# A hybrid decoder layer on one Trainium2 core: the prompt's mLSTM packed into five tiles of one projection, six of that projection's tiles as Strassen pairs, operand sums in two passes

## The chip, the cores and the metric

The kernel runs on one core of one Trainium2 chip. The metric is device time in microseconds of one launch; three runs of the kernel before gave a median of 2462.95 us. One further execution was profiled, and every duration in the prediction comes from it.

A core has TensorE (PE; PEld is its weight load), VectorE (DVE), ScalarE (ACT), GpSimd (POOL) and SyncE (SP), which here only issues DMA transfers. POOL issues DMA transfers too. Each engine works through its own queue in order and waits there for what its next instruction needs. SBUF is the memory on the chip, PSUM its accumulator memory, eight banks of which TensorE writes and VectorE and ScalarE read.

## What is computed

One inference step of one layer, for a prompt of 512 tokens and a batch of 8 × 4 sample tokens, in fp32. Cut to what matters here:

```python
def _merge(x, h_m, o_m, z_m, h_a, z_a, g_m, g_a, ...):
    ...
    br_m = hn.reshape(B, T, M_WIDTH) * jax.nn.sigmoid(o_m) * jax.nn.silu(z_m)
    br_a = h_a * jax.nn.silu(z_a)
    y = (jax.nn.sigmoid(g_m) * jnp.einsum('btc,cd->btd', br_m, w_proj_m)
         + jax.nn.sigmoid(g_a) * jnp.einsum('btc,cd->btd', br_a, w_proj_a))
    out = jnp.einsum('btc,cd->btd', y, w_out)
    return _layernorm(DN_ALPHA * x + out, ln_w, ln_b)
```

The step first multiplies the 544 tokens by `w_in` (2048 × 18952), which yields q, k, v of two branches and all gates. The attention branch gives `h_a` (sliding window, sinks), the mLSTM branch gives `h_m`: per head (four, of width 512) scores of keys and queries under exponential decays, their product with the values, a normaliser, a layernorm, and the new matrix memory C. Then come three 2048 × 2048 projections: `w_proj_a` on the attention branch, `w_proj_m` on the mLSTM branch, and `w_out` on the gated sum.

## The kernel before

All activations lie with channels on the 128 partitions and the 544 tokens along the free axis. To keep fp32 precision, each operand of a product is split into a high part (a cast to fp32r by ScalarE, line 200 for weights, 245 for activations) and a low part (source minus high part, by VectorE, lines 201 and 246), and a product is three matmuls: high × high, high × low, low × high.

A *plain* tile (`gemm`, line 224, with `products`, line 205) makes 128 output columns. It loads two halves of weights (512 KB each, in three buffers `raw`), splits them, and runs 16 k × 3 matmuls × 2 column halves of 272 tokens = 96 matmuls into two PSUM banks from the pool `psA`. Every so many k (`every`) it calls `tick()`, which lets each of the background generators in `live` trace its next step at that place of the program.

A *Strassen pair* (`paired`, line 718) makes two tiles with seven products of half size in place of eight. Each product (`half_product`, line 677) is 16 + 8 matmuls into one bank. `prepare` (line 658) makes the sums of weights, some on VectorE and some by accumulating DMA transfers from POOL, and splits them; `gather` (line 689) collects the results, partly on POOL (line 704). The right-hand operands of a pair are four quarters of the activations and four sums of quarters, called s1, n2, n3 and s4: products 1 and 2 (counted from 0) use s1 and n2, products 4 and 5 use n3 and s4.

The order of instructions on each engine is made when the program is built, by a scheduler with its own model of durations: each instruction has a priority by its place in the program, `tc.high_priority(offset)` moves it ahead, and `tc.issue_after` ties it behind another one.

The part in question is the last quarter of the time. The branch `d_bra` is split into 8 activation tiles (`branch`, line 1367). Then 16 plain tiles of `w_proj_a` run (line 1555), each loading its gate `d_sga`, multiplying the result by it (line 1560) and storing to `d_t`. Beside them the prompt's mLSTM is a background generator (`mlstm`, line 1506) with one step in each tick, two k apart. For each head it transposes the values (`values`, line 1414) and keys (`keys`, line 1422) through PSUM tiles of the pool `psB`, makes C (line 1438), the scores (line 1470), the weighted values (line 1483), a layernorm, and turns the rows back (line 1493) into `d_brm`. Both PSUM pools hold four banks. When the mLSTM is done, its SBUF is closed, and `d_brm` is read back and split beside the remaining plain tiles.

Then the projection by `w_proj_m`: four plain tiles, five pairs, two plain tiles. Beside the four plain tiles `operand_sums` (line 1574) makes the sums of quarters. It has eight items; an item k loads rows k and k + 8 of the source (544 KB, a transfer issued by POOL, line 1578) into one of two buffers `tx`, makes four sums on VectorE (lines 1587 to 1590) and splits each (four casts, four subtractions of 272 columns), with two ticks to an item. The load for item k + 2 is traced after item k. The projection by `w_out` begins the same way, with sums of `d_y` (line 1674).

Of the kernel before, what the change touches and what calls it, by code (L numbers as in the profile page):

```python
# [25 lines left out]
T = SEQ + NS  # L26
# [48 lines left out]
def _build(tc, nc, i, o, es):  # L75
# [3 lines left out]
    def pool(stack, name, bufs, space=None, side=None):  # L79
        kw = {"space": space} if space is not None else {}  # L80
        if space is None:
            kw["side"] = side or "right"
            kw["reuse_waits"] = "tile"
        return stack.enter_context(tc.tile_pool(name=name, bufs=bufs, **kw))
# [9 lines left out]
    psB = pool(es, "psB", 4, PSUM)  # L94
    psA = pool(es, "psA", 4, PSUM)

    dr = pool(es, "dr", 1, bass.MemoryType.DRAM)
# [3 lines left out]
    def nm(s):  # L101
        count[0] += 1
        return f"{s}_{count[0]}"

# [71 lines left out]
    d_y = dr.tile([16, 128, T], F32, name="d_y")  # L176
    d_o = dr.tile([12, 128, T], F32, name="d_o")
# [46 lines left out]
    def gemm(wv, c0, xh, xl, cols=EVEN, raws=(None, None), every=8, prio=0, before=None, parts=(1, 1),  # L224
             ps=None, behind=None):
        ps = ps or mm()
        for half in range(2):
# [9 lines left out]
            products(ps, half, wh, wl, xh, xl, cols, every)  # L237
# [480 lines left out]
    def paired(work, plain=None):  # L718
# [6 lines left out]
        for at, (w, n) in enumerate(steps):  # L725
# [11 lines left out]
            if n == 2 and "early" in w:  # L737
                w["early"]()
            half_product(w, n)
# [642 lines left out]
    _, bah, bal, g_ = branch(d_bra, act, lambda k: ev(), ahead)  # L1382
# [18 lines left out]
    def f5(dt=F32):  # L1401
        return wA2.tile([128, 512], dt, tag="f5", name=nm("f"))

# [18 lines left out]
    def keys(h, c, kt):  # L1422
# [19 lines left out]
        V.tensor_copy(co[:, 256:512], p1[:, 0:256])  # L1442
# [19 lines left out]
    def cells(h, kh, kl, qh, ql):  # L1462
        hns = []
        for bs_ in ((0,), (1,), (2, 3)):
# [10 lines left out]
            yield  # L1475
        for js in ((0, 1), (2,), (3,)):
            for j in js:
# [9 lines left out]
                hns.append(hn)  # L1487
            yield
        gt = load4(d_g, h)
# [16 lines left out]
    def mlstm():  # L1506
        for h in range(MH):
            vts = load4(d_v, h)
            spawn(decays(h))
            yield  # L1510
            kts = load4(d_k, h)
# [3 lines left out]
            kh, kl, qh, ql = [], [], [], []  # L1515
            g_ = None
            for c in range(4):
                a, b_ = t5(F32R), t5(F32R)
                V.tensor_copy(a[:], kts[c][:])
                V.tensor_tensor(out=b_[:], in0=kts[c][:], in1=r32(a[:]), op=ALU.subtract)  # L1520
                kh.append(a)
                kl.append(b_)
                n_ = keys(h, c, kts[c])
                next(n_)
                if g_ is not None:
# [4 lines left out]
            for c in range(4):  # L1530
                a, b_ = t5(F32R), t5(F32R)
                hilo(qts[c][:], a[:], b_[:])
                qh.append(a)
                ql.append(b_)
# [3 lines left out]
            yield from cells(h, kh, kl, qh, ql)  # L1538
# [15 lines left out]
    bmh = None  # L1554
    for ct in range(16):
        sg = c5t()
        nc.sync.dma_start(sg[:], d_sga[ct])
        ps = gemm(wa_, ct * 128, bah, bal, every=2)
        for p_, s_ in halves(ps, sg):
            V.tensor_tensor(out=s_, in0=p_, in1=s_, op=ALU.mult)  # L1560
        nc.sync.dma_start(d_t[ct], sg[:])
        if bmh is None and (not live or ct == 15):
            drain()
            esA.close()
            es3, esE = ExitStack(), ExitStack()
            act3 = pool(es3, "act3", 8)
            bm_, bmh, bml, g_ = branch(d_brm, act3, lambda k: c5t() if k % 2 else ev())
            spawn(g_)
            c6 = pool(esE, "c6", 2)
            esR = ExitStack()  # L1570
            wr2, pe_ = pool(esR, "wr2b", 3), pool(esR, "peb", 1)
            tx = pool(esR, "txb", 2)
    drain()
    def operand_sums(src, to, p):

        def load(k):
            t_ = tx.tile([128, 2, T], F32, tag="tx", name=nm("tx"))
            G.dma_start(out=t_[:], in_=src[k:k + 9:8].rearrange("k p t -> p k t"))
            return t_

# [353 lines left out]
```

## Time and profile before

| what | value |
|---|---|
| three runs: median (lowest to highest) | 2462.95 us (2462.81 to 2464.43) |
| the profiled execution: its time / its span | 2464.16 us / 2462.4 us |
| mean granted TensorE clock | 0.997 |
| HBM traffic | 169 GB/s over the span |

The chain of work that ended last, by engine (shares of the span) and the costliest lines of it:

```profile
PE 94%; DMA 3%; DVE 2%; issue 1%; ACT 1%; SPq 0%; DVEq 0%; POOL 0%; ACTq 0%; POOLq 0%
```

How to read the rows: times are microseconds unless marked ns, and count from the start of the span. A group row has the line of the kernel, the engine, the operation, `out<-in` by the program's names, shapes, the count; then busy time and mean ns of one; then the idle time of the engine just before these instructions and what ended it (`<-`). A timeline row has start, length, engine, line, operation; idle time before it stands in brackets. Matmuls overlap: one that lasts 0.29 us starts 0.125 us after the one before.

### The profile page before, as it was taken

What the parts mean: (1) busy time and instruction counts of PE and PEld (TensorE: products, weight loads), DVE (VectorE), ACT (ScalarE), POOL (GpSimd) and SP (SyncE); (2) the same over time, 40 slices, a digit from 0 to 9 for tenths busy, and PEclk for the clock granted to TensorE, in tenths of its full rate; (3) what the DMA queues carried; (4) which work ended last, traced back from release to release, by engine and by line L of the source; (5) the groups of instructions that cost most, each with busy time, mean ns of one, the idle gap of its engine ahead of it and who ended that gap; (6) DMA issues with size and microseconds to landing.
All of it is one profiled execution on the core that took longest, in us unless ns stands there. A gap on an engine that the chain in (4) does not pass through costs nothing.

```text
span 2462.4 us, 48812 instructions
## 1 busy us (share of the span) xinstructions
PE 2433.8 (99%) x19446; PEld 2378.9 (97%) x19446; DVE 1884.0 (77%) x2813; ACT 1215.4 (49%) x1994; POOL 509.9 (21%) x478
## 2 busy tenths in 40 slices
PE   8999999999999999999999999999999999999997
PEld 8999999999999999999999999999999999999996
DVE  7768888888888887787887888878855654767657
ACT  5456676676676564433433444544633333344431
POOL 3114334334333331211121122210000000110111
PEclk9999999999999999999999999999999999999998
DMA  6866666666666644578587687576755546888876
GB/s 177 201 173 158 163 161 144 162 161 150 160 154 160 155 124 138 143 217 247 179 242 244 163 241 229 176 251 217 246 171 173 187 147 210 226 218 253 220 221 188
DMA packets 557436, 464.72 MB, mean 189 GB/s; under 512 B 45592, under 2 KB 454344, under 8 KB 556952
## 3 DMA queue, kind: packets, MB, share of 16 engines
q1 hardware_dynamic: 540312, 402.09, 55.1%
q0 software_dynamic: 15696, 57.15, 12.1%
q8 instruction: 153, 2.51, 0.4%
q10 hardware_dynamic: 1200, 2.36, 0.3%
q14 instruction: 75, 0.61, 0.1%
HBM read 319.06 MB, written 96.31 MB: 169 GB/s over the span
## 4 chain that ended last, share of the span: by engine, by line
PE 94%; DMA 3%; DVE 2%; issue 1%; ACT 1%; SPq 0%; DVEq 0%; POOL 0%; ACTq 0%; POOLq 0%
PE bank L685 46%; PE bank L687 23%; PE bank L210 11%; PE sm L1438 2%; PE sm L210 1%; PE bank L1250 1%; PE sm L1470 1%; PE sm L795 1%; PE sm L1483 1%; PE sm L841 1%; DMA tx<-d_y 1%; DMA ty<-d_y 1%; DMA raw<-in_w_in 1%; PE sm L1800 1%; PE sm L821 1%
## 5 line engine op out<-in xcount | busy, mean ns | idle before, releaser
L200 ACT CAST wh<-raw 128x1024 fp32r<-128x1024 f32 x632 | 662.7, 1049 | 836.2 <-PE bank L685 686.6
L201 DVE TENSOR_TENSOR wl<-raw,wh 128x1024 fp32r<-128x1024 f32 x632 | 792.2, 1255 | 194.6 <-ACT wh L200 175.3
L685 PE MATMUL bank<-xk,wh 128*128 128x272 f32 x2336 | 322.7, 289 | 0.0
L665 DVE TENSOR_TENSOR raw<-raw,raw 128x1024 f32<-128x1024 f32 x238 | 304.1, 1279 | 12.6 <-DMA raw<-in_w_in 8.3
L685 PEld LDWEIGHTS bank<-xk,wh 128*128 128x128 f32 x2336 | 303.0, 188 | 2.8 <-issue 2.4
L704 POOL TENSOR_TENSOR ev<-p,ev 128x272 f32<-128x272 f32 x82 | 117.9, 1438 | 458.3 <-ACT ev L703 401.2
L685 PE MATMUL bank<-n2h,wh 128*128 128x272 f32 x656 | 169.8, 291 | 0.2 <-ACT wh L200 0.2
L687 PE MATMUL bank<-xk,wl 128*128 128x272 f32 x1168 | 169.7, 288 | 0.0
L685 PE MATMUL bank<-n3h,wh 128*128 128x272 f32 x656 | 169.6, 291 | 0.0
L685 PE MATMUL bank<-s1h,wh 128*128 128x272 f32 x656 | 169.1, 291 | 0.0
L685 PE MATMUL bank<-n2l,wh 128*128 128x272 f32 x656 | 167.7, 288 | 0.0
L685 PE MATMUL bank<-n3l,wh 128*128 128x272 f32 x656 | 167.6, 288 | 0.0
L685 PE MATMUL bank<-s1l,wh 128*128 128x272 f32 x656 | 167.3, 287 | 0.0
L685 PE MATMUL bank<-s4h,wh 128*128 128x272 f32 x656 | 167.2, 289 | 0.0
L685 PE MATMUL bank<-s4l,wh 128*128 128x272 f32 x656 | 167.0, 287 | 0.0
L687 PEld LDWEIGHTS bank<-xk,wl 128*128 128x128 f32 x1168 | 155.6, 188 | 0.1
L685 PE MATMUL bank<-a11h,wh 128*128 128x272 f32 x584 | 150.6, 290 | 0.0
L685 PE MATMUL bank<-a11l,wh 128*128 128x272 f32 x584 | 149.4, 288 | 0.0
L210 PE MATMUL bank<-bh,wl 128*128 128x272 f32 x704 | 147.5, 290 | 0.7 <-DVE wl L201 0.7
L210 PE MATMUL bank<-bh,wh 128*128 128x272 f32 x704 | 148.1, 289 | 0.0
L210 PE MATMUL bank<-bl,wh 128*128 128x272 f32 x704 | 148.0, 289 | 0.0
L663 POOL DMA_DIRECT2D raw<-raw x90 | 78.1, 868 | 291.8 <-DVE ev L712 202.2
(493 smaller groups left out, 5670.4 us busy)
## 6 DMA issues: line engine op xcount, KB each, us to landing
raw<-in_w_in SPq DMA_DIRECT2D x296, 512.0 KB
raw<-raw POOLq DMA_DIRECT2D x90, 512.0 KB, 4.8
C<-in_state_mlstm_C SPq DMA_DIRECT2D x32, 1024.0 KB
out<-C SPq DMA_DIRECT2D x64, 512.0 KB
raw<-in_w_proj_a SPq DMA_DIRECT2D x32, 512.0 KB
raw<-in_w_proj_m SPq DMA_DIRECT2D x32, 512.0 KB
raw<-in_w_out SPq DMA_DIRECT2D x32, 512.0 KB
d_v<-ev SPq DMA_DIRECT2D x16, 272.0 KB
```

The lines of the kernel that those rows point to most:

```text
L200: state["cast"] = A.copy(wh[:, k:k + n], raw[:, k:k + n])
L201: state["split"] = V.tensor_tensor(out=wl[:, k:k + n], in0=raw[:, k:k + n], in1=r32(wh[:, k:k + n]), op=ALU.subtract)
L210: PE.matmul(ps[f][:, :w], a[:, kk], b(k, c, w), start=(k == 0 and n == 0), stop=(k == 15 and n == 2))
L663: G.dma_start(out=w[out][:], in_=w[b][:], accum_op=ALU.add)
L665: V.tensor_tensor(out=w[out][:], in0=w[a][:], in1=w[b][:], op=ALU.add)
L685: PE.matmul(ps, wh[:, k], x(p, k), start=(first and k == 0 and p == 0), stop=False, skip_group_check=True)
L687: state["end"] = PE.matmul(ps, wl[:, k], x(0, k), start=False, stop=(k == 7), skip_group_check=True)
L704: G.tensor_tensor(out=c22, in0=p1, in1=c11, op=ALU.subtract)
L795: PE.matmul(pp[:, c0 + w0:c0 + 256], qs[a][:, j * 128:j * 128 + 128], kx[:, k0:k0 + 256 - w0], start=(n == 0), stop=(n == 1))
L821: PE.transpose(pt[:, b * 128:b * 128 + 128], s_[:, b, 128:256], ident)
L841: PE.matmul(po[:, b * 128:b * 128 + n], VA[:, b], p_[:, 2 * b:2 * b + n // 128], start=(b == 0 and m == 0), stop=(b == 3 and m == 1), skip ...
L1438: PE.matmul(pp[:, 0:258], a[:, b * 128:b * 128 + 128], b_[:, b, f], start=(b == 0 and n == 0), stop=(b == 3 and n == 2))
```

## The change

PSUM pools can be closed and opened anew: six banks for `psB` and two for `psA` from the start of the `w_proj_a` projection on, four and four again before its pairs. The mLSTM runs beside the first five tiles, with a tick after every k in the first half of a tile and after every second k in the second half. Its loads of the next head's v and k and of the gate are traced earlier, its output rows become a generator of their own (`rows_out`) that runs beside the next head, two of its VectorE copies become ScalarE's, and one step of waiting is dropped. Three plain tiles follow (5 to 7) with the operand sums of `d_bra` beside them, then three pairs (tiles 8 to 13), then two plain tiles (14 and 15) with the reading back of `d_brm`. `operand_sums` has sixteen items in two passes: the first makes n2 and s1 from a full load and stores n2 to `d_n2` in HBM; the second loads three parts again, n2 among them, and makes n3 and s4. Each item is two sums, one cast and one subtraction of 544 columns. It is also the form used for `w_proj_m` and `w_out`, with one tick to an item.

```diff
+    def psum_pools(n):
+        return pool(esPS, nm("psB"), n, PSUM), pool(esPS, nm("psA"), 8 - n, PSUM)
...
-    def paired(work, plain=None):
+    def paired(work, plain=None, rest=()):
...
+            if at == 4:
+                for _ in rest:
+                    pass
             half_product(w, n)
...
+    esPS.close()
+    psB, psA = psum_pools(6)
...
         A.copy(co[:, 0:256], p0[:, 0:256])
-        V.tensor_copy(co[:, 256:512], p1[:, 0:256])
+        A.copy(co[:, 256:512], p1[:, 0:256])
...
+        if h + 1 < MH:
+            pre["v"] = load4(d_v, h + 1)
+        gt = load4(d_g, h)
         for js in ((0, 1), (2,), (3,)):
...
+            if js[-1] == 3 and h + 1 < MH:
+                pre["k"] = load4(d_k, h + 1)
+            yield
+        spawn(rows_out(h, hns, gt))
+
+    def rows_out(h, hns, gt):
...
+            def two_parts(src, to):
+                a, b_ = t5(F32R), t5(F32R)
+                hilo(src[:], a[:], b_[:])
...
-                V.tensor_copy(a[:], kts[c][:])
-                V.tensor_tensor(out=b_[:], in0=kts[c][:], in1=r32(a[:]), op=ALU.subtract)
...
+                two_parts(kts[c], (kh, kl))
...
+    def operand_sums(src, to, p, pace=1):
+        e, f = ([[p.tile([128, 4, 2, HT], F32R, tag="act", name=nm("sum" + n)) for _ in range(2)] for n in "hl"]
+                for _ in range(2))
...
+        def load(k):
+            t_ = tile4()
+            G.dma_start(out=t_[:].rearrange("p (a c) t -> p a (c t)", a=2), in_=src[k:k + 9:8].rearrange("k p t -> p k t"))
+            return t_
+
+        def again(k):
+            t_ = tile4()
+            G.dma_start(out=t_[:, 0:2].rearrange("p c t -> p (c t)"), in_=src[k])
+            G.dma_start(out=t_[:, 2], in_=src[k + 8][:, 0:HT])
+            G.dma_start(out=t_[:, 3], in_=d_n2[k])
+            return t_
+
+        work = [(load, k) for k in range(8)] + [(again, k) for k in range(8)]
+        ahead = [load(0), load(1)]
+        for n, (of, k) in enumerate(work):
+            for _ in range(pace if n < 12 else 1):
+                yield
+            t_ = ahead.pop(0)
+            if of is load:
+                V.tensor_tensor(out=t_[:, 3], in0=t_[:, 3], in1=t_[:, 1], op=ALU.subtract)
+                V.tensor_tensor(out=t_[:, 0], in0=t_[:, 0], in1=t_[:, 3], op=ALU.subtract)
+                nc.sync.dma_start(d_n2[k], t_[:, 0])
+                hilo(t_[:, 0:4:3], e[0][k // 4][:, k % 4], e[1][k // 4][:, k % 4])
+            else:
+                V.scalar_tensor_tensor(t_[:, 1], t_[:, 0], -1.0, t_[:, 1], op0=ALU.mult, op1=ALU.subtract)
+                V.tensor_tensor(out=t_[:, 2], in0=t_[:, 2], in1=t_[:, 3], op=ALU.subtract)
+                hilo(t_[:, 1:3], f[0][k // 4][:, k % 4], f[1][k // 4][:, k % 4])
+            if n + 2 < len(work):
+                nxt, k_ = work[n + 2]
+                ahead.append(nxt(k_))
...
+        return dict(wv=wa_, x=XA, cA=ct * 128, cB=ct * 128 + 128, scale=1.0, acc=True, end=end, early=early)
+
+    LEAD_A, PAIR_A, TAIL_A = 5, 8, 14
+    for ct in range(LEAD_A):
+        plain_a(ct, every=(1, 2))
     drain()
...
+    tx = pool(esR, "txb", 2)
+    SA = {}
+    sums_ = operand_sums(d_bra, SA, act3, 2)
+    next(sums_)
+    spawn(sums_)
+    for ct in range(LEAD_A, PAIR_A):
+        plain_a(ct, every=2, prio=AHEAD)
+    esPS.close()
+    psB, psA = psum_pools(4)
+    XA = operands((bah_, bal_), SA)
+    paired([pair_a(ct) for ct in range(PAIR_A, TAIL_A, 2)], state["split"], rest=sums_)
+    state["end"] = None
+    drain()
+    bm_, bmh, bml, g_ = branch(d_brm, act3, lambda k: ev() if k % 5 < 3 else c6t())
+    spawn(g_)
+    for ct in range(TAIL_A, 16):
+        plain_a(ct, every=2, prio=AHEAD)
+    drain()
```

More of the change, by code (lines that the diff above doesn't have):

```diff
@@ L1556, in _build, with operands, c6t, plain_a @@
+    def operands(tiles, sums):
+        low = [t[2:] for t in tiles]
+        return [side_by_side(tiles, 0), sums["s1"], sums["n2"], side_by_side(low, 0),
+                sums["n3"], sums["s4"], side_by_side(low, HT)]
+    def c6t():
+        return c6.tile([128, T], F32, tag="c6", name=nm("c6"))
+    def plain_a(ct, **kw):
         sg = c5t()
[L1557 to L1558 removed]
+        with tc.issue_after(state["load"].ins):
+            nc.sync.dma_start(sg[:], d_sga[ct])
+        ps = gemm(wa_, ct * 128, bah, bal, **kw)
```

105 lines of the change are left out of this document (45 added, 60 removed).

## The prediction

> **What bounds the kernel now.** I read the page's busy shares first, then the windows by stage, then TensorE's own order of time.
>
> ```profile
> span 2462.4 us, 48812 instructions
> ...
> PE 2433.8 (99%) x19446; PEld 2378.9 (97%) x19446; DVE 1884.0 (77%) x2813; ACT 1215.4 (49%) x1994; POOL 509.9 (21%) x478
> ```
>
> The windows cut the part that the change touches: tiles 0 to 10 of the attention projection with the mLSTM beside them, the rest of that projection, then the four plain tiles of the second and of the third projection with operand sums beside them. Columns: stretch, length, busy time of each engine (instructions), granted clock, share of the DMA engines, GB/s.
>
> ```profile
> 1757.10:2014.10 257.00, 256.30 (x2041) 253.91 (x2040) 161.10 (x401) 99.28 (x190) 10.62 (x20) 1.00 0.53 176
> 2014.10:2078.50 64.40, 64.40 (x520) 64.40 (x519) 30.38 (x46) 22.17 (x31) 0.00 (x0) 1.00 0.70 214
> 2078.50:2126.70 48.20, 48.20 (x387) 48.20 (x386) 35.45 (x72) 18.05 (x35) 5.29 (x7) 1.00 0.78 232
> 2256.70:2305.00 48.30, 47.55 (x382) 47.33 (x381) 37.18 (x78) 22.91 (x49) 5.26 (x7) 1.00 0.82 229
> ```
>
> TensorE idles 0.7 us in the first, nothing in the second and third, 0.75 us in the last. So here time is won only by fewer matmuls and lost by whatever makes TensorE wait.
>
> **Step 1: the matmuls that go.** The timeline of TensorE shows a Strassen product (16 + 8 matmuls) and then plain ones:
>
> ```profile
> 1754.07 2.17 PE L685 MATMUL bank<-xk,wh 128*128 128x272 f32 x16
> 1756.07 1.17 PE L687 MATMUL bank<-xk,wl 128*128 128x272 f32 x8
> 1757.08 0.41 PE L210 MATMUL bank<-bh,wh 128*128 128x272 f32 x2
> ...
> 2077.60 0.41 PE L210 MATMUL bank<-bh,wh 128*128 128x272 f32 x2
> 2077.84 0.41 PE L210 MATMUL bank<-bl,wh 128*128 128x272 f32 x2
> 2078.09 0.42 PE L210 MATMUL bank<-bh,wl 128*128 128x272 f32 x2
> 2078.35 0.41 PE L210 MATMUL bank<-bh,wh 128*128 128x272 f32 x2
> ```
>
> A product takes 1757.08 − 1754.07 = 3.01 us, so a pair (seven) 21.07. Six plain matmuls take 0.75 us, so a tile (96) 12.03 with the 125.4 ns of the product's matmuls, and two tiles 24.07. Three pairs save 3 × 3.0 = **9.0 us**. A pair's VectorE work is seven splits, two weight sums, four gathers and two gate products. With VectorE's durations of lines 201, 1560 and 246 in the next fence that is 9 × 1.22 + 4 × 0.43 + 2 × 0.72 = 14.1 us in 21, hidden; uncovered it would cost 14.1 − 6.6 (the four splits and four evacuations of two plain tiles) = 7.5 us a pair.
>
> **Step 2: the mLSTM in five tiles.** The last stretch of the projection holds 64.4 / 12.03 = 5.35 tiles, the first 10.65, or 128 us; the mLSTM's own TensorE time is thus 257 − 128 = 129 us. Five tiles and the mLSTM: 60 + 129 = 189 us. VectorE's 161 us of the first stretch hold 21 weight splits and gate products, of which five tiles keep ten; 11 × (1.22 + 0.43) = 18 us go, and so do the groups of lines 1442 and 1519 below, which move to ScalarE (6.8 and 6.7):
>
> ```profile
> L201 DVE TENSOR_TENSOR wl<-raw,wh 128x1024 fp32r<-128x1024 f32 x33 | 40.2, 1219 | 18.7 <-ACT wh L200 18.6
> ...
> L1560 DVE TENSOR_TENSOR c<-bank,c 128x272 f32<-128x272 f32 x32 | 12.6, 430 | 12.4 <-PE bank L210 12.2
> ...
> L1442 DVE COPY f<-sm 128x256 f32<-128x256 f32 x16 | 6.8, 422 | 24.1 <-PE sm L1438 24.1
> ...
> L1519 DVE CAST t<-t 128x512 fp32r<-128x512 f32 x16 | 6.7, 420 | 1.5 <-DMA t<-d_k 1.5
> ...
> L246 DVE TENSOR_TENSOR bl<-ev,bh 128x544 fp32r<-128x544 f32 x8 | 5.6, 720 | 1.5 <-ACT bh L245 1.4
> ...
> L245 ACT CAST bh<-ev 128x544 fp32r<-128x544 f32 x8 | 5.0, 647 | 4.0 <-DMA ev<-d_brm 3.9
> ```
>
> About 130 of 189 us stay on VectorE and at most 99 + 14 on ScalarE: covered, cost 0. The loads of the next head's v and k go out earlier on SP's queue and may wait there for tiles, with weights behind them; a half of weights is wanted only every 19 us there, so 0 again, and a few us if that slack goes.
>
> **Step 3: two banks for a plain tile.** The bank pool falls from four to two for tiles 0 to 7, and a tile needs two. The next tile cannot start until VectorE has read both: 0.29 us to the end of the last matmul, two reads of 0.43, and on average half a 1.2 us split in front, less 0.125 of overlap: 1.3 us. At the ends of tiles 0 to 4 an mLSTM step stands between (24 matmuls of an output block, or a score block), and hides it. Tiles 5 and 6 have only operand sums beside them: 2 × 1.3 = **2.6 us**. Bounds: 0, if VectorE's reads come just in time, to 7 × 1.9 = 13 (all seven ends, a whole split in front). [...]
>
> **Step 4: operand sums in sixteen items instead of eight, on the same two buffers.** This decides. It happens three times: new for the attention projection, and changed for the second and third projections, where the pace rises from one item in two ticks (6 us) to one in each (3 us). Old items, in the tile view, and what a load takes:
>
> ```profile
> L1587 DVE TENSOR_TENSOR tx<-tx x16: 429/441/444, 1965.4 to 2298.6; 128x272 f32<-128x272 f32 x16
> ...
> L245 ACT CAST s1h<-tx x16: 413/420/422, 2068.6 to 2299.1; 128x272 fp32r<-128x272 f32 x16
> ...
> DMA to landing us min/median/max: 3.9/6.3/9.0
> ...
> tx<-d_brm POOLq DMA_DIRECT2D x8, 544.0 KB, 6.8
> ...
> tx<-d_y POOLq DMA_DIRECT2D x8, 544.0 KB, 5.2
> ```
>
> With two buffers a load starts only when the item two before it is done. POOL's timeline in the third projection shows that: each load was held by the last sum of the item in its buffer, and the chain of waits runs through the loads.
>
> ```profile
> 2265.50 0.72 POOL L1578 DMA_DIRECT2D tx<-d_y  x1 [8.82 <-DVE s4l L246]
> 2267.48 0.72 POOL L1578 DMA_DIRECT2D tx<-d_y  x1 [1.26 <-DVE s4l L246]
> 2275.83 0.72 POOL L1578 DMA_DIRECT2D tx<-d_y  x1 [7.63 <-DVE s4l L246]
> 2278.95 0.72 POOL L1578 DMA_DIRECT2D tx<-d_y  x1 [2.40 <-DVE s4l L246]
> ...
> 2265.50 7.81 DMA tx<-d_y x2
> ...
> 2278.95 14.23 DMA tx<-d_y x2
> ```
>
> So a buffer's cycle was 10.3 and 11.5 us, and two items came out of each. The new cycle, from rows: landing 5.2 (the lower of the two medians), start 0.2, two VectorE operations 0.9, then a 544-wide cast 0.65 and subtraction 0.72 with 0.2 of hand-over. In the first pass the store of the partial sum must land before the buffer is free; no row gives a 136 KB store, so I bound it by 1.6 (hidden behind cast and subtraction) and 5.2 (a load four times as large), and take 3.3, in between, because it is smaller than the load but starts on SP's queue behind weight loads. First pass 5.2 + 0.2 + 0.9 + 3.3 = 9.6. In the second pass three transfers replace one, POOL's issues 0.72 each, of which I charge one: 5.2 + 0.7 + 0.2 + 0.9 + 1.6 = 8.6. Two items are loaded ahead and take 3.5; then three cycles of the first and four of the second kind: 3.5 + 28.8 + 34.4 = **66.7 us** for a set of sums. With 3.9 for the landing and the store hidden it is 3.5 + 3 × 6.6 + 4 × 7.3 = 52.5; with 6.8 and 5.2 it is 3.5 + 3 × 13.1 + 4 × 10.2 = 83.6.
>
> When must it be done? The fifth product of the first pair reads the last of the second pass, at its eighth k, 1.75 us in. In the second and third projections that is 48.2 + 4 × 3.01 + 1.75 = 62 us after the first plain matmul. In the second projection the low parts go where the old operand's high parts of k 8 to 11 lie, which are read until a quarter before the end of the last tile, 3 us before: 66.7 − 3 − 62 = 1.7 us of waiting. In the third the first sum came 3.2 us after the stage's start:
>
> ```profile
> 2259.89 0.43 DVE L1587 TENSOR_TENSOR tx<-tx 128x272 f32<-128x272 f32 x1
> ```
>
> 66.7 + 3.2 − 62 = 7.9. In the attention projection only three plain tiles lie ahead, 36.1 + 2.6 + 12.0 + 1.75 = 52.5 after the mLSTM's tiles come free: 66.7 − 52.5 = 14.2. Together **23.8 us**. Where the wait appears I leave open: at the fifth product, or earlier, if VectorE stands at a late load with weight splits behind it; either way the set's length is what counts. Bounds of the sum: 0 (52.5 each), and 31 + 19 + 25 = 75 (83.6 each).
>
> [...]
>
> **Step 5: what moves at no charge.** Each set loads 544 KB eight times more and stores 136 KB eight times, 5.6 MB: over 62 us 90 GB/s on top of 230, which is why I don't take the shortest landing. POOL's queue gets the second-pass loads among the pair's accumulating transfers and the subtraction that waits for ScalarE:
>
> ```profile
> POOL ev L704 <- ACT ev L703: 401.2, 53, 22.8
> ```
>
> A load behind that wait is late too; it's inside the upper bound. The mLSTM's gated branch is read back in tiles 14 and 15: 16 × (0.65 ScalarE, 0.72 VectorE), 11.5 us of VectorE in 24 beside four splits and evacuations, hidden, since the plain tiles of the next projection want its k one by one.
>
> **The sum.** The profiled execution took 2464.16 us (span 2462.4 and 1.8 around it), 1.2 above the median of the runs. 2464.2 − 9.0 + 2.6 + 23.8 = 2481.6; less 1.2: **2480 us**, 0.7% slower.
>
> **Rivals.** *The loads keep up (faster).* If landing stays near its 3.9 and the store hides, a set takes 52.5 us and nobody waits: 2463 − 9.0 + 2.6 = 2457. For it: shorter VectorE work per item (2 operations and one wide subtraction for 3.5 us of eight), and the attention stage moves fewer bytes now (0.70 share). Against: the old third set, at half the pace, already had its chain of waits in the loads. It decides from a mean cycle below about 7.2 us (of 9.0 in my sum), and is the case on the other side.
>
> *Half of it (no change).* Cycles between 7.2 and 8.2 us: at 7.9 the attention projection alone waits, 58.8 − 52.5 = 6.3 us, and the gain is spent: 2463. For it: the medians include loads beside many others. Against: my 9.0 leaves nothing for the weight splits that stood between the sums of the old sets.
>
> *The mLSTM does not fit.* A head now takes 63 us, the distance of its score blocks in the chain of waits:
>
> ```profile
> 1796.30 7.54 PE sm L1470 x48
> ...
> 1859.62 7.59 PE sm L1470 x48
> ```
>
> It would get 189 / 4 = 47. If the chain scores, layernorm, transposes needs 50, its tiles are freed 12 us later, and the new sums with them; TensorE goes on with plain tiles but meets the sums 12 us later: 2480 + 12 = 2492. For it: small VectorE and POOL steps in a row. Against: the next head's loads and the row output now overlap it.
>
> *Fewer products don't appear*, since seven for eight are counted in the code: no chance given.
>
> **Chances.** Loads too slow (forecast) 0.49; mLSTM late as well 0.10; half 0.13; loads keep up 0.28. A run of this kernel tells about 0.2% (5 us) from no change. Faster 0.28, same 0.13, slower 0.59. The forecast's own range is 2467 to 2500 (mean cycles of 8.2 to 10, seven to a set). The range to hold the time reaches down to the gain kept whole, 2454, and up to 2500, leaving out cycles beyond 10 us in all three sets.
>
> **What would show it.** Right: TensorE idle in the attention projection's first pair, ended by casts or subtractions of n3 or s4, 10 us or more; POOL's second-pass loads held by the item two before; set lengths (first sum to last subtraction) near 67 us. Step 1 is right if the pairs' products stand at 3.01 us, step 3 if gaps of about 1.3 us end on VectorE's gate product. Wrong: TensorE without gaps at the first pairs, set lengths under 55 us, or idle time inside tiles 0 to 4.

## The result and the profile after

The kernel with the change takes 2537.9 us (four runs, 2536.4 to 2538.3) against 2463.7 before: ratio 1.030, 95% interval 1.0282 to 1.0318. It is slower, as forecast, but by 74 us and not by 17, and outside the range of 2454 to 2500.

The page of the changed kernel, span and busy shares:

```profile
span 2536.1 us, 49009 instructions
...
PE 2454.0 (97%) x19374; PEld 2388.0 (94%) x19374; DVE 1914.3 (75%) x2818; ACT 1244.9 (49%) x2028; POOL 564.4 (22%) x567
```

TensorE has 72 matmuls fewer, three pairs with one product of 24 matmuls saved in each, and is busy 20 us longer. Fewer matmuls in more time is a matter of the granted clock, 0.66 to 1.00 in the windows that follow. Columns as in the prediction. A projection ends here with its last store. The rows are the attention projection in three parts (up to its first pair, the first pair, the rest), then the second projection, then the third with the end of the kernel:

```profile
1757.00:1990.00 233.00, 228.62 (x1811) 225.37 (x1811) 145.97 (x367) 108.81 (x220) 13.01 (x22) 1.00 0.58 188
1990.00:2050.00 60.00, 33.98 (x160) 27.47 (x159) 31.25 (x52) 15.31 (x22) 19.81 (x32) 0.66 0.67 198
2050.00:2121.00 71.00, 69.06 (x553) 68.84 (x552) 44.59 (x60) 30.69 (x43) 6.91 (x7) 1.00 0.86 246
2121.00:2310.00 189.00, 180.78 (x1416) 179.13 (x1416) 127.82 (x181) 71.80 (x91) 32.47 (x45) 0.99 0.88 248
2310.00:2536.00 226.00, 194.44 (x1431) 190.24 (x1429) 135.57 (x204) 65.09 (x87) 36.32 (x50) 0.92 0.74 211
```

The second and third projection of before (the rows of its attention projection stand in the prediction, 257.00 + 64.40 = 321.4 us):

```profile
2078.50:2258.70 180.20, 180.20 (x1442) 180.20 (x1441) 126.84 (x191) 73.44 (x105) 21.70 (x23) 1.00 0.84 235
2258.70:2462.00 203.30, 185.98 (x1439) 184.04 (x1437) 136.11 (x220) 67.38 (x103) 24.16 (x26) 0.97 0.74 208
```

The attention projection is 42.6 us longer (233 + 60 + 71 = 364 against 321.4), the second 8.8, the third 22.7. Counted by matmuls, some 4 us of the 42.6 belong to the second projection: the last matmul of tile 15 ends at about 2116 and its store stands at 2120.9, where before it was 2077.6 and 2078.5. The second row is the one to see: in the 60 us of the first pair TensorE did 160 matmuls, which at the 125.4 ns of before take 20 us. Of the 40 us lost, 26 are idle, and 14 went into matmuls at a granted clock of 0.66. The waits of TensorE say what it stood for (us in total, times, longest):

```profile
PE bank L692 <- ACT sumh L252: 29.6, 14, 4.8
PE bank L217 <- DVE wl L208: 8.6, 6, 3.3
PE bank L692 <- ACT wh L207: 6.6, 4, 2.2
PE bank L692 <- DVE suml L253: 5.5, 8, 1.5
...
PE bank L217 <- DVE c L1630: 0.5, 1, 0.5
```

The high and low parts of the operand sums end 35 us of waiting in all, and the casts and splits of weights another 15, in plain tiles (217) and in products (692): in the second projection all waits, 8.3 us, are of this second kind. There VectorE stood at a sum whose load had not landed, with the weight splits behind it, and ScalarE at the cast of that sum, with a cast of weights behind it. One such place (first VectorE, then ScalarE), after which TensorE waits 0.76 us for a split at 2123.45:

```profile
2119.30 0.44 DVE L1603 TENSOR_TENSOR tx<-tx 128x272 f32<-128x272 f32 x1 [4.37 <-DMA tx<-d_brm]
...
2120.26 0.65 ACT L252 CAST sumh<-tx 128x544 fp32r<-128x544 f32 x1 [7.75 <-DVE tx L1604]
2120.81 1.05 ACT L207 CAST wh<-raw 128x1024 fp32r<-128x1024 f32 x1
```

VectorE's gate product, for which the prediction gave 2.6 us, ends one gap of 0.5.

How long a set of sums took is in the tile view of its subtractions (duration in ns, first and last start), one row for each projection:

```profile
L253 DVE TENSOR_TENSOR suml<-tx,sumh x16: 714/724/726, 1970.9 to 2039.8; 128x544 fp32r<-128x544 f32 x16
...
L253 DVE TENSOR_TENSOR suml<-tx,sumh x16: 718/720/726, 2111.8 to 2190.5; 128x544 fp32r<-128x544 f32 x16
...
L253 DVE TENSOR_TENSOR suml<-tx,sumh x16: 716/719/726, 2314.1 to 2391.0; 128x544 fp32r<-128x544 f32 x16
```

From the first subtraction to the end of the last (in the third projection from the first sum, at 2311.3), 70, 79 and 80 us; the forecast was 67, with bounds of 52.5 and 83.6. In the first two projections the sums of the first two items had been made long before (from 1762.8 and 2042.5 on) and waited for memory. POOL's timeline of the third projection shows why (start, duration, in brackets the idle time before and what ended it; line 1586 is a load of the first pass):

```profile
2315.79 0.72 POOL L1586 DMA_DIRECT2D tx<-d_y  x1 [8.13 <-DVE suml L253]
2317.67 0.72 POOL L1586 DMA_DIRECT2D tx<-d_y  x1 [1.16 <-DMA d_n<-tx]
2327.77 1.44 POOL L1586 DMA_DIRECT2D tx<-d_y  x2 [9.38 <-DMA d_n<-tx]
2341.40 1.44 POOL L1586 DMA_DIRECT2D tx<-d_y  x2 [12.19 <-DMA d_n<-tx]
```

Two loads go out every 12 to 13.6 us, and what they wait for is the store of the partial sum out of the buffer (`d_n<-tx`). The prediction gave this cycle 9.6 us. In the chain of waits (start, length, what ran) loads and stores alternate in the first pass:

```profile
1972.66 7.04 DMA tx<-d_bra
1979.70 8.92 DMA d_n<-tx
...
1998.06 1.74 DMA d_n<-tx
...
2322.86 4.34 DMA d_n<-tx
...
2333.98 6.85 DMA d_n<-tx
```

Six stores stand in the chain; they held their buffers for 1.7, 1.7, 2.3, 4.3, 6.9 and 8.9 us. The prediction put in 3.3, with bounds of 1.6 and 5.2. Around the longest (1979 to 1990) the DMA engines moved 274 GB/s, around the first of the two shortest (1997 to 2001) 111.

### The profile page after: what moved, and what is told of

It reads as the page before. It is cut to its first block, busy times and chain, and to the rows that moved or that the text cites. A ratio compares the mean times of both kernels' runs of the same rounds, so it can differ in the third digit from the quotient of the medians.

```text
span 2536.1 us, 49009 instructions
## 1 busy us (share of the span) xinstructions
PE 2454.0 (97%) x19374; PEld 2388.0 (94%) x19374; DVE 1914.3 (75%) x2818; ACT 1244.9 (49%) x2028; POOL 564.4 (22%) x567
## 4 chain that ended last, share of the span: by engine, by line
PE 85%; DMA 8%; issue 3%; DVE 2%; ACT 1%; POOL 0%; DVEq 0%; SPq 0%; POOLq 0%; ACTq 0%
PE bank L692 45%; PE bank L694 23%; PE bank L217 3%; PE sm L1451 2%; DMA tx<-d_n 2%; PE bank L1260 1%; PE sm L217 1%; DMA tx<-d_y 1%; PE sm L1483 1%; PE sm L805 1%; PE sm L1499 1%; PE sm L851 1%; DMA tx<-d_brm 1%; DMA d_n<-tx 1%; DMA tx<-d_bra 1%
## 5 line engine op out<-in xcount | busy, mean ns | idle before, releaser
L670 POOL DMA_DIRECT2D raw<-raw x96 | 83.6, 871 | 307.2 <-DVE ev L719 203.3
L692 PE MATMUL bank<-n2h,wh 128*128 128x272 f32 x584 | 151.2, 291 | 0.4 <-ACT wh L207 0.4
L692 PE MATMUL bank<-n3h,wh 128*128 128x272 f32 x584 | 151.0, 291 | 0.0
L692 PE MATMUL bank<-s1h,wh 128*128 128x272 f32 x584 | 150.7, 291 | 0.0
L692 PE MATMUL bank<-n2l,wh 128*128 128x272 f32 x584 | 149.3, 287 | 0.0
L692 PE MATMUL bank<-n3l,wh 128*128 128x272 f32 x584 | 149.2, 287 | 0.0
L692 PE MATMUL bank<-s1l,wh 128*128 128x272 f32 x584 | 148.9, 287 | 0.0
L692 PE MATMUL bank<-s4l,wh 128*128 128x272 f32 x584 | 148.5, 287 | 0.0
L692 PE MATMUL bank<-sumh,wh 128*128 128x272 f32 x384 | 103.1, 306 | 35.8 <-ACT sumh L252 29.6
L217 PE MATMUL bank<-bh,wl 128*128 128x272 f32 x512 | 113.3, 293 | 5.4 <-DVE wl L208 5.4
L217 PE MATMUL bank<-bh,wh 128*128 128x272 f32 x512 | 112.3, 291 | 2.1 <-ACT wh L207 1.6
```

Source lines behind the costliest of these rows:

```text
L217: PE.matmul(ps[f][:, :w], a[:, kk], b(k, c, w), start=(k == 0 and n == 0), stop=(k == 15 and n == 2))
L670: G.dma_start(out=w[out][:], in_=w[b][:], accum_op=ALU.add)
L692: PE.matmul(ps, wh[:, k], x(p, k), start=(first and k == 0 and p == 0), stop=False, skip_group_check=True)
```

## The experiments

The suspects: the cover of the first set, the extra pass (its loads, its store, its VectorE work), the number of buffers, the two banks, and the mLSTM's packing. The first four kernels take one of these each. Plain tiles only in the attention projection, one-pass sums in the others:

```diff
-    for ct in range(LEAD_A, PAIR_A):
-        plain_a(ct, every=2, prio=AHEAD)
     esPS.close()
     psB, psA = psum_pools(4)
-    paired([pair_a(ct) for ct in range(PAIR_A, TAIL_A, 2)], ...)
+    for ct in range(LEAD_A, TAIL_A):
+        plain_a(ct, every=2, prio=AHEAD)
...
-    sums_ = operand_sums(d_brm, M, act)
+    spawn(operand_sums_1(d_brm, M, act))
```

> Only the packing is left: the mLSTM in five tiles, all sixteen tiles plain, no sums of the attention branch, and the old one-pass sums for the other two projections. Theory (the sets of operand sums cost the time, the packing is nearly free): 2463 plus the 5 us by which the first eight tiles of the changed kernel ran over, about 2468. Rival (the packing itself costs much, by stalls or by a late mLSTM): 2480 or more. Rival (two banks and new orders matter on their own): in between.

2486.6 us, 1.0085 (1.007 to 1.010): the rival's number. But it told little about the packing: the four-bank pools are opened anew ahead of tile 5 here, and tile 5 waited for that. The store of tile 4 stands at 1920.8, that of tile 5 at 1983.4. Two later kernels (below) replace it.

The changed kernel with one-pass sums in the second and third projections only (`operand_sums_1` is the function of before):

```diff
-    sums_ = operand_sums(d_brm, M, act)
+    spawn(operand_sums_1(d_brm, M, act))
...
-    sums_ = operand_sums(d_y, Y, act3)
+    spawn(operand_sums_1(d_y, Y, act3))
```

> The changed kernel with the old one-pass sums (eight items, two ticks each) in the second and third projections. Theory: these two stages, 189.0 and 226.1 us in the changed kernel against 180.1 and 203.8 before, come back, and the rest stays: 2538 - 31 = 2507. Rival (they were slow because they inherit something from the attention projection, such as a late read-back of the mLSTM branch or a low clock): less than 15 us come back, 2523 or more.

2508.2 us, 1.0171 (1.0156 to 1.0186), as expected: the second pass costs 1.030 − 1.0171, or 32 us, in these two projections, where the change had nothing to gain.

No store and no reload of the partial sum; it is taken from its two parts in SBUF, with one more subtraction to an item of the second pass:

```diff
-            G.dma_start(out=t_[:, 3], in_=d_n2[k])
...
-                nc.sync.dma_start(d_n2[k], t_[:, 0])
...
-                V.tensor_tensor(out=t_[:, 2], in0=t_[:, 2], in1=t_[:, 3], op=ALU.subtract)
+                for part in e:
+                    V.tensor_tensor(out=t_[:, 2], in0=t_[:, 2], in1=r32(part[k // 4][:, k % 4, 0]), op=ALU.subtract)
```

> The second pass takes n2 from its two parts in SBUF (two subtractions in place of one), so the store to HBM in the first pass and one of the three reloads go. Theory A (the store holds the buffers: POOL waited for it 34.5 us in five places): 10 us less in each set, 2505 to 2515. Theory B (two buffers and the length of a load set it, with or without the store): within 10 us of 2538.

2530.6 us, 1.0263 (1.0248 to 1.0279). The sets fall to 68, 71 and 73 us, but no further, and the time by 9: the store that stands in the chain of waits is a small part of the set's length. With it gone, VectorE still stood 24.2, 20.5 and 21.9 us for loads into the same buffers in the three sets.

Two plain tiles more ahead of the pairs, so 24 us more of cover:

```diff
-    LEAD_A, PAIR_A, TAIL_A = 5, 8, 14
+    LEAD_A, PAIR_A, TAIL_A = 5, 10, 14
```

> The changed kernel with two more plain tiles in front of the pairs of the attention projection (pairs from tile 10, two pairs). Theory (the first pair waits only because its sums are not done): 24 us more cover take as much from a wait of about 40, and one pair's gain of 3 us is lost: 2538 - 21 = 2517. Rival (the pairs stall by themselves: queues, low clock, accumulating transfers): 2530 or more.

2534.3 us, 1.0278 (1.0261 to 1.0295), a miss: the projection ends 6.9 us earlier and not 20. The set grew with its cover:

```profile
L253 DVE TENSOR_TENSOR suml<-tx,sumh x16: 717/718/727, 1975.0 to 2054.8; 128x544 fp32r<-128x544 f32 x16
```

It takes 81 us beside plain tiles instead of 70 beside a TensorE that waits for it. VectorE's waits for the loads of the sums were the same in both (26.0 us of the 80 from 1975 on, 25.8 of the 70 from 1970 in the changed kernel). What grew is its own work (40.1 us against 35.0) and its waits for ScalarE's weight casts (7.9 against 0.8), so the longer set is not shown to come from slower transfers. The added tiles also stood behind the sums: once VectorE waited for a load with a gate product behind it, and TensorE stopped for 7.3 us, since a plain tile had only two banks:

```profile
1996.46 0.44 DVE L1603 TENSOR_TENSOR tx<-tx 128x272 f32<-128x272 f32 x1 [3.98 <-DMA tx<-d_bra]
...
1997.45 0.78 DVE L1630 TENSOR_TENSOR c<-bank,c 128x272 f32<-128x272 f32 x2
...
1998.03 0.57 PE L217 MATMUL bank<-bh,wh 128*128 128x272 f32 x1 [7.32 <-DVE c L1630]
```

A set's length is no constant, and cover bought with TensorE's work lengthened it.

The next four. One-pass sums everywhere with the pairs from tile 10, then from tile 8, and plain tiles alone with the bank pools of the change (six for the mLSTM, two for the tile, until tile 8):

```diff
-    sums_ = operand_sums(d_bra, SA, act3, 2)
+    sums_ = operand_sums_1(d_bra, SA, act3)
...
-    LEAD_A, PAIR_A, TAIL_A = 5, 8, 14
+    LEAD_A, PAIR_A, TAIL_A = 5, 10, 14
```

> One-pass sums (eight items, one load each) in all three projections, and the attention projection's pairs only from tile 10 (two pairs, five plain tiles of cover). Theory (the number of load cycles against the cover decides): a set of eight takes about 43 us from 1972, so it ends at 2015, where the first pair is due to begin at about 2011: a wait of 0 to 4 us, 6 us gained by two pairs, 4 to 6 us lost to the packing: 2461 to 2468. Rival (sums beside the packed tiles are slow for another reason, such as VectorE's order): 2480 or more.

> One-pass sums everywhere, pairs from tile 8 as in the changed kernel. Theory: the set ends at 2015 instead of 2041, the first pair waits some 24 us from 1991 on instead of more than 40; all gains of three pairs stay: about 2484, against 2508 with two passes in the attention projection alone. Rival (the second pass's loads are not what costs): 2500 or more.

```diff
-    paired([pair_a(ct) for ct in range(PAIR_A, TAIL_A, 2)], state["split"], rest=sums_)
+    for ct in range(PAIR_A, TAIL_A):
+        plain_a(ct, every=2, prio=AHEAD)
```

> As the run with only the packing, but the PSUM pools stay at six and two banks until tile 8, as in the changed kernel, so that plain tiles can run on beside the end of the mLSTM. Theory: the 22 us of that run came from the pools, which were opened anew at tile 5 and held the next tiles back until the mLSTM's last tiles were free; without this the packing costs 4 to 6 us: about 2468. Rival (the packing itself costs 20 us): 2480 or more.

From tile 10: 2478.6 us, 1.005 (1.0038 to 1.0063). From tile 8: 2490.6 us, 1.010 (1.0086 to 1.0113). No pairs: 2474.4 us, 1.0033 (1.0021 to 1.0045). All three are over what was expected (2461 to 2468, 2484, 2468), by some 6 to 10 us each, which pointed to something that all share. Between them: three pairs on one-pass sums make the kernel 16 us slower than none, since the set, now 41 us long, still has not enough cover (TensorE waits 13 us for sums); two pairs later make it 4 slower, a difference that the two intervals barely carry. With pairs from tile 10 TensorE's waits in the stretch end otherwise:

```profile
PE bank L217 <- DVE c L1656: 3.1, 2, 2.6
PE bank L692 <- DVE ev L713: 2.9, 1, 2.9
```

Of 7.7 us in all none is for a sum. Line 1656 is the gate product that empties a plain tile's banks: it stands behind the sums in VectorE's order (ten of them straight ahead of the one that held TensorE for 2.6 us). So sums that came in time still held a tile that had only two banks.

Three buffers and three loads ahead for the sums of the third projection alone:

```diff
-        ahead = [load(0), load(1)]
+        ahead = [load(k) for k in range(deep)]
...
-    tx = pool(esT, "txd", 2)
+    tx = pool(esT, "txd", 3)
...
-    sums_ = operand_sums(d_y, Y, act3)
+    sums_ = operand_sums(d_y, Y, act3, deep=3)
```

> The changed kernel with three buffers instead of two, and three loads ahead, in the sums of the third projection only. Theory (two buffers and the length of a load set the pace): three items come out of a cycle instead of two, the set of 16 shrinks by about a third, and the third projection's 226 us fall to about 210: 2522. Rival (bandwidth, or VectorE's order of splits and sums): less than 5 us gained, 2533 or more.

2524.8 us, 1.0239 (1.0225 to 1.0253). The set of that projection:

```profile
L253 DVE TENSOR_TENSOR suml<-tx,sumh x16: 714/720/726, 2320.8 to 2381.7; 128x544 fp32r<-128x544 f32 x16
```

64 us from its first sum at 2318.0, against 80, with the same loads, stores and VectorE work: what the set waits for is a free buffer, and a third one alone brings back 15 of the 23 us that this projection lost. With an unchanged turnaround (the time from one load of a buffer to the next) three buffers for two would have made it 54, so the turnaround itself grew.

Then three kernels. The kernel before with the two-pass function (here under the name `operand_sums`) in its second and third projections and nothing else of the change:

```diff
-    spawn(operand_sums(d_brm, M, act))
+    sums_ = operand_sums(d_brm, M, act)
+    next(sums_)
+    spawn(sums_)
...
-    spawn(operand_sums(d_y, Y, act3))
+    sums_ = operand_sums(d_y, Y, act3)
+    next(sums_)
+    spawn(sums_)
```

> The kernel before with nothing changed but the sums of the second and third projections, which take the two-pass form. Theory (the form costs its time wherever it stands): the same 31 us as between the changed kernel and the one with one-pass sums there: 2465 + 31 = 2496. Rival (these two stages were slow only behind the changed attention projection): 2480 or less.

2497.7 us, 1.0136 (1.0121 to 1.0151): 33 us, as the removal had given 32. This loss is independent of the rest.

Both passes, but neither store nor second loads; the second pass takes its operands from what SBUF holds, high parts only, so this kernel leaves out the low parts in n3 and s4:

```diff
-            G.dma_start(out=t_[:, 0:2].rearrange("p c t -> p (c t)"), in_=src[k])
-            G.dma_start(out=t_[:, 2], in_=src[k + 8][:, 0:HT])
-            G.dma_start(out=t_[:, 3], in_=d_n2[k])
...
-                nc.sync.dma_start(d_n2[k], t_[:, 0])
...
+                up, dn = (r32(tiles[0][q // 4][:, q % 4]) for q in (k, k + 8))
```

> As the run without the store, and the second pass loads nothing either: it reads the high parts of the operands that lie in SBUF (the low parts are left out of n3 and s4, so the output is not the reference's; number and size of VectorE's and ScalarE's operations stay). Theory (the loads set the length of a set): the second pass falls from 32 us to about 18 in each set, and 25 to 40 us of the 2531 go: 2490 to 2505. Rival (VectorE's order, with splits in between, sets it): less than 10 us, 2520 or more.

2492.1 us, 1.0114 (1.0097 to 1.0131). From the kernel without the store, 1.0263, the second loads are 37 us, one subtraction to an item included, which the other kernel had more. The sets of the second and third projections fall to 45 and 53 us, and these two projections to 385.1 us from the last store of the attention projection to the end of the span, against 415.2 with the change and 383.9 before. The kernel with one-pass sums everywhere and pairs from tile 8 took 1.010, so two passes as such, with their VectorE work, are nearly free in all three projections; reading everything again is not.

Plain tiles with the packing and four banks for each all along:

```diff
-    esPS.close()
-    psB, psA = psum_pools(6)
...
-    esPS.close()
-    psB, psA = psum_pools(4)
```

> Only the packing, with four and four banks all along (no pools opened anew). The same kernel with six and two banks until tile 8 took 2474 against 2466 before. If the two banks of a plain tile cost most of those 8 us, this run takes 2467 or less. If the mLSTM's own chains cost them, fewer of its tiles in PSUM make it no faster: 2472 or more.

2464.6 us, 1.000 (0.9991 to 1.0009): the packing itself costs nothing and gives nothing. Against the same with six and two banks this is 8 us. The waits of TensorE in the attention projection, first of this kernel, then of the one with two banks:

```profile
PE bank L217 <- DVE wl L208: 0.7, 1, 0.7
```

```profile
PE bank L217 <- DVE c L1656: 2.4, 2, 1.9
PE sm L1451 <- issue: 2.3, 1, 2.3
PE sm L1451 <- ACT kwh L252: 1.7, 1, 1.7
```

Gaps at the gate product are 2.4 us of the 8. The mLSTM's own products (line 1451) have 4.0. The rest is clock, in the first 43 us of the projection (four banks first, then two):

```profile
1757.00:1800.00 43.00, 42.30 (x331) 41.60 (x330) 27.10 (x44) 25.41 (x51) 0.21 (x2) 1.00 0.64 205
```

```profile
1757.00:1800.00 43.00, 40.02 (x297) 39.10 (x297) 27.14 (x45) 25.79 (x51) 0.21 (x2) 0.96 0.65 210
```

At 0.96 some 1.7 us of 43 are lost. That with four banks matmuls of a plain tile fill the mLSTM's waits is my reading of the 34 matmuls more. The price of four banks is that the mLSTM ends later: its last rows are stored at 1996.7, against 1968.5 in the changed kernel.

Last, one pair alone: four and four banks, one-pass sums everywhere, tiles 12 and 13 as the pair. Against the kernel just shown nothing else changes; the loads five steps ahead in the third projection, of which the expectation speaks, are not in it.

```diff
-    LEAD_A, PAIR_A, TAIL_A = 5, 8, 14
+    LEAD_A, PAIR_A, TAIL_A = 5, 12, 14
...
+    sums_ = operand_sums_1(d_bra, SA, act3)
+    next(sums_)
+    spawn(sums_)
...
-    for ct in range(PAIR_A, TAIL_A):
-        plain_a(ct, every=2, prio=AHEAD)
+    paired([pair_a(ct) for ct in range(PAIR_A, TAIL_A, 2)], state["split"], rest=sums_)
```

> The packing with four and four banks all along, one-pass sums everywhere, loads five steps ahead in the third projection, and only the last two of the tiles before the plain ones as a pair (tiles 12 and 13, one plain tile after it). In e11 the mLSTM's last rows stand at 1997 and tile 11's last store at 2030, so the only pair is due to begin at about 2030. Theory (a pair costs nothing where its set has its cover): a one-pass set took 42 us in e6, so it ends at about 2039 if it starts at 1997; the pair's products use it in order, so it waits 4 to 5 us at most against the 3.0 us that a pair saves: 2461 to 2467, a ratio of 0.999 to 1.002. Rival (a pair in this projection costs something of its own, whatever its cover): more than 2470, a ratio over 1.003, with waits of the products on the sums although they started 30 us ahead.

2473.6 us, 1.0035 (1.0022 to 1.0049): the rival's number. The sums began at 2004, 30 us ahead of their first use at 2034.5, and the last came at 2047. TensorE's windows around the pair:

```profile
1757.00:2030.00 273.00, 271.66 (x2163) 268.99 (x2162) 167.54 (x410) 121.99 (x247) 12.83 (x23) 1.00 0.59 186
2030.00:2070.00 40.00, 34.52 (x240) 33.07 (x239) 31.81 (x57) 19.73 (x32) 5.17 (x6) 0.91 0.73 214
```

and its waits in the projection:

```profile
PE bank L217 <- ACT wh L207: 1.7, 1, 1.7
PE bank L692 <- ACT s1h L252: 1.5, 1, 1.5
PE bank L692 <- DVE s1l L253: 1.4, 2, 1.1
```

The 240 matmuls of these 40 us are 30 us of work: 5.5 idle and 4.4 at a low clock (0.91 on the mean) are lost for the 3.0 that a pair saves. Three of the idle microseconds are for sums, 2.4 for casts of weights. The projection ends at 2087.6 and not at 2077.9; some 2 us of that 9.7 I cannot place. That the set is to blame, for time on VectorE and in the queues which the tiles and the pair need, is my reading; whether a pair with its sums wholly done beforehand still costs something was not tried, nor a third buffer in this projection, whose memory would have to come from another pool. No kernel of the study beats the one before.

## Why the direction was right and the size wrong

The loss adds up from these ratios, each difference times 2463 us:

| part | from, to | us |
|---|---|---|
| packing | 1.000, 1.000 | 0 |
| two banks until tile 8 | 1.000, 1.0033 | +8 |
| three pairs on one-pass sums (−9.0 inside) | 1.0033, 1.010 | +16.5 |
| second pass in the attention projection | 1.010, 1.0171 | +17.5 |
| second pass in the two others | 1.0171, 1.030 | +32 |
| together | | +74 |

The scheduler orders each kernel anew, so a row is the difference of two kernels and need not stand in the changed kernel with the same size: up to 1990 that one has 3.7 us more idle time than before, and not 8.

**Step 1, the matmuls that go: right.** The timeline of TensorE in an undisturbed pair after the change has its low-part groups 3.01 us apart:

```profile
2067.77 1.17 PE L694 MATMUL bank<-bh,wl 128*128 128x272 f32 x8
2070.79 1.16 PE L694 MATMUL bank<-bh,wl 128*128 128x272 f32 x8
```

**Step 2, the mLSTM in five tiles at no cost: right in price, wrong in what it means for the start of the sums.** This is the step that failed first. I took the mLSTM's 129 us of TensorE time and five tiles, and had its memory come free as tile 5 starts, 52.5 us ahead of the sums' last due time. But the mLSTM is a chain, and TensorE takes plain tiles while it waits. Its score blocks in the chain of waits after the change:

```profile
1792.10 7.59 PE sm L1483 x48
...
1944.49 6.87 PE sm L1483 x45
```

A head takes (1944.5 − 1792.1) / 3 = 51 us and not 47, so tile 5 and more than half of tile 6 were done when its memory came free at 1970, after the last rows; the first product of the pairs starts at 1986.5. The cover was 1986.5 + 4 × 3.01 + 1.75 − 1970.2 = 30 us, not 52.5, against a set of 70. My rival *The mLSTM does not fit* named that chain (50 us a head, tiles 12 us late) and gave it a chance of 0.10; it came about, with 22 us for its 12. That the same tiles which keep TensorE busy eat the cover was in its last clause ("goes on with plain tiles but meets the sums 12 us later"), and the forecast itself left it out. One of the prediction's signs of being wrong came with it: 3.1 us of idle time inside tiles 0 to 4, at the mLSTM's products.

**Step 3, two banks: mis-sized.** 2.6 us forecast, 8 measured; gaps at tiles 5 and 6 of the changed kernel come to 0.5. (The terms that the prediction names for one gap add up to 1.6 us and not 1.3, so 3.3 for two.) I looked for the loss in reads at tile ends, which are 2.4 of the 8, in two gaps. The rest are waits in the mLSTM's products (4.0) and the clock (0.96 in the first 43 us, some 1.7); that with two banks no plain tile can run ahead into these waits is my reading.

**Step 4, the sets: the mechanism right, the first pass too short.** 66.7 us were forecast from a cycle of 9.0; the sets of the second and third projections took 79.4 and 80.4, a cycle of (80 − 3.5) / 7 = 10.9. A cycle of the first pass in the third projection took 12.0 and 13.6 us for 9.6, one of the second pass about 9.3 for 8.6. For the 0.2 of start and the 0.2 of hand-over in a cycle the prediction has no row, they were my estimate; in the chain of waits after the change two sums started 0.08 us behind their loads (2320.70 to 2320.78, 2332.95 to 2333.03), and in the chain before it a subtraction 0.02 us behind its cast (2278.19 to 2278.21). The stores took 1.7 to 8.9 us and not 3.3, and the 544 KB loads of these two sets landed after medians of 6.2 and 6.1 us, not after the 5.2 I took as the lower median. Put into the prediction's own formula the measured lengths give 79.4 − 3 − 62 = 14 us for the second projection (8.8 measured, some 13 with the 4 us of matmuls that ran ahead) and 80.4 + 1.3 − 62 = 20 for the third (22.7), so its due times were fair. Measured less forecast (1.7 and 7.9) the two are 22 us. The bound of 83.6 for a set held; the range left such cycles out by its last clause. That all of the 8.8 + 22.7 = 31.5 us come from the two-pass form is shown twice, by taking it away (32) and by adding it alone (33).

**The wait's place.** I expected TensorE to stand at the fifth product, for n3 and s4. It stood from the second product of the first pair on: with the cover so short, the first pass itself was late, and 10.8 us of the 26 were waits for s1 and n2 (up to 2010). The other 15.2 were waits for n3 and s4, where I expected them, and near the 14.2 of the forecast; that the size fits is luck, since the cover was 22 us shorter than forecast. The longest wait of each kind, in TensorE's timeline:

```profile
1996.21 0.52 PE L692 MATMUL bank<-sumh,wh 128*128 128x272 f32 x2 [4.55 <-ACT sumh L252]
...
2022.71 0.82 PE L692 MATMUL bank<-sumh,wh 128*128 128x272 f32 x2 [4.85 <-ACT sumh L252]
```

**Step 5, nothing for the extra traffic: not shown to be wrong.** The second loads cost 37 us together with the buffers they hold; it is where the time of the second pass lies. But the full loads landed no later than before on the whole (medians of 6.2 and 6.1 us, against 6.8 and 5.2), and with the same traffic a third buffer brought back 15 of the 23 us. How much of the rest is traffic was not told apart.

**The sum.** It had no term for the clock. Of the 42.6 us of the attention projection 31.6 are more idle time (32.3 against 0.7 in the windows) and 9.0 are saved, so TensorE was busy 20 us longer with the rest: 14 in the 60 us of the first pair, where the clock was 0.66, and some 4 with matmuls of the second projection that ran ahead of the last store. A wait there cost about one and a half times its length (40 us lost, 26 idle).

## What to carry to other kernels

A set of preparatory work fed through two buffers took about its turnaround times its items over two here, and the turnaround was longer than forecast beside everything else that ran (10.9 us for 9.0): before splitting the set into two passes, count how often each buffer turns, because a second read of everything cost 37 us here where the second pass without it cost next to nothing (1.0114 against 1.010, some 3 us). Cover is to be counted from the moment memory really comes free to the moment of use, with what fills the waits meanwhile taken out; work that TensorE pulls forward shortens the cover of whatever comes behind (30 us here for 52.5). Saved matmuls are worth their time only where the operands they need instead are ready without new waits, and a wait is to be priced with the slow clock that can come with it (40 us lost here for 26 idle).

## What the runs showed of the hardware

The granted clock fell with TensorE's waits here far enough to be a term of the sum (0.66 in the 60 us of the first pair). Windows of 10 us around the first pair of the changed kernel:

```profile
1980.00:1990.00 10.00, 10.00 (x83) 10.00 (x82) 6.35 (x9) 4.34 (x5) 0.73 (x1) 1.00 0.93 268
...
2030.00:2040.00 10.00, 4.84 (x13) 3.11 (x13) 4.84 (x10) 1.93 (x3) 3.97 (x7) 0.50 0.44 144
2040.00:2050.00 10.00, 10.00 (x62) 9.74 (x63) 7.96 (x12) 3.56 (x4) 1.66 (x2) 0.77 0.63 175
```

With 13 matmuls in 10 us the clock is 0.50, and when work is back after 2040 without gaps the mean of the next 10 us is still 0.77. How short a wait it may take is seen in the kernel with one pair, in windows of 1 us, behind a gap of 1.75 us that ended at 2058.0:

```profile
2058.00:2059.00 1.00, 1.00 (x6) 0.84 (x7) 1.00 (x4) 0.00 (x0) 0.00 (x0) 1.00 1.01 329
2059.00:2060.00 1.00, 1.00 (x7) 1.00 (x6) 1.00 (x2) 0.51 (x1) 0.00 (x0) 0.54 0.53 184
2060.00:2061.00 1.00, 1.00 (x6) 1.00 (x6) 1.00 (x2) 0.88 (x3) 0.00 (x0) 0.50 0.02 9
2061.00:2062.00 1.00, 1.00 (x7) 1.00 (x6) 1.00 (x3) 0.55 (x1) 0.00 (x0) 0.50 0.14 35
2062.00:2063.00 1.00, 1.00 (x8) 1.00 (x8) 0.38 (x1) 0.57 (x1) 0.00 (x0) 0.76 0.80 220
2063.00:2064.00 1.00, 1.00 (x10) 1.00 (x10) 0.47 (x2) 0.48 (x1) 0.00 (x0) 1.00 1.15 355
```

The clock was 1.00 in the first microsecond after work was back, 0.50 to 0.76 in the next four, and 1.00 again from 2063 on. TensorE's timeline has 22 matmuls from 2059.05 to 2063.33, 4.28 us for what 125.4 ns each make 2.76: the slow spell cost 1.5 us, nearly as much again as the gap. The length of a gap does not settle it. In the kernel with one-pass sums and pairs from tile 10 a gap of 2.60 us that ended at 2005.5 left the clock at 1.00 in the windows on both sides of 2010, and the 2.9 us of idle time between 2030 and 2040 went with 0.83:

```profile
2000.00:2010.00 10.00, 7.39 (x59) 7.20 (x58) 8.23 (x19) 3.84 (x9) 1.07 (x2) 1.00 0.39 122
2010.00:2020.00 10.00, 10.00 (x83) 10.00 (x82) 4.79 (x9) 2.87 (x5) 1.35 (x2) 1.00 0.71 208
...
2030.00:2040.00 10.00, 7.14 (x45) 6.95 (x44) 6.99 (x13) 2.49 (x3) 0.00 (x0) 0.83 0.68 176
```

What decides between the two is not shown.
